# Expert blocks of 128 rows in three float32r passes, with weights split slice by slice into a ring

## The chip, the cores and the metric

The kernel runs on one core of one Trainium2 chip. The metric is device microseconds of one execution. Engines are named as in the profile: PE (TensorE) with its weight loads PEld, DVE (VectorE), ACT (ScalarE), POOL (GpSimd), SP (SyncE, which issues most transfers).

## The reference

One layer of an encoder for 1024 tokens of width 1024, all float32: a mixer sub-layer (neighbourhood attention, bidirectional RWKV-7 and pooling, side by side), then a mixture of experts: 32 experts in 4 groups, two per token.

```
u  = layer_norm(x1) * (1 + scale2) + shift2
# 2048 (token, expert) pairs, sorted by expert, padded per expert to blocks
hb = silu(xb @ w_gate[e]) * (xb @ w_up[e])      # 1024 -> 512, one expert per block
yb = (hb @ w_down[e]) * wt                      # 512 -> 1024, wt = router weight
f  = segment_sum(yb)                            # two rows of y for each token
x  = layer_norm(ALPHA * x1 + gate2 * f) * gain + bias
```

## The kernel before

The program has three parts. The mixer and the router (to about 958 us) are laid out by a scheduler. The expert stage (to about 1540) and the last stage (to the end) are written by hand, each engine with its own program and semaphores, in `experts` and `tail_plan`.

**The expert stage** works through blocks of one expert's tokens. A block holds up to 128, 64 or 32 rows; its size (3, 2 or 1, and 0 behind the last) is read from `m_code` at run time (L1499), and `by_size` (L1513) puts each piece of code in three `If`s, one per size. In this input 37 blocks run: 14 of 128 rows, 5 of 64, 18 of 32. Two blocks of 128 rows follow each other at four places; the others stand between smaller ones. `go_on` (L1523) branches out of the program behind the last block, from the sixteenth on.

The order on every engine is that of `pipeline`: for block g the head of g, the rows of g+1, the down product of g-1, the turn of g.
- *Rows*: POOL gathers a block's rows of u by index into one of NX = 4 buffers `m_xg` (L1612). PE transposes them (L1655); ACT and DVE each move one half into `m_xT` (`evac_T`, L1721).
- *Head*: PE forms gate and up products in `m_pgu`, for 128 rows in two halves of 256 columns (L1672), for smaller blocks several parts of the array at a time (L1680). ACT takes SiLU (L1748, L1751), DVE multiplies (L1772, L1776).
- *Turn*: PE transposes h (L1688), ACT copies it to `m_hT` (L1756).
- *Down*: PE forms `m_py` (L1700, L1711). DVE multiplies by the channel's gate (`out`, L1734, L1739) into one of NY = 3 buffers, and POOL scatters the rows to `ys` (L1620). The router's weight comes in later.

SP loads the three weight matrices of each block (2 MB each) into one of NB = 3 buffers `w`, where the expert changes, gated on the head (semaphore `gu1`) and the down product (`y1`) of the block three before. Behind the last block `finish` loads x1, gain and bias; when POOL has seen its scatters land it signals `done`, and SP then loads `ys`.

**The last stage** has eight tiles of 128 tokens. For each, PE adds two rows of `ys`, weighted by diagonal matrices `dg`, and ALPHA*x1 by a third diagonal, 12 records a tile (L1804). Even tiles get their variance by DVE's `bn_stats` (L1813), odd ones by ACT's copies with sums and squares (L1834, L1841); L1817 is the mean, L1821 and L1826 the small steps to the scale, L1849 and L1852 the normalisation, and DVE applies gain and bias (L1829, L1830). SP writes each tile out.

In the mixer a float32r split already exists: ACT casts a weight tile to `w_h` (L189), DVE subtracts for `w_l` (L190), and three products follow (L196 to L198).

Of the kernel before, what the change touches and what calls it, by code (L numbers as in the profile page):

```python
# [18 lines left out]
D = 1024  # L19
# [8 lines left out]
NB, NPRE, NX, NY, NP = 3, 3, 4, 3, 50  # L28
# [5 lines left out]
def _consts():  # L34
# [18 lines left out]
    add("alpha", np.float32(ALPHA) * np.eye(128))  # L53
# [70 lines left out]
class Builder:  # L124
# [905 lines left out]
    def phase3(self, p3, wo, mk, ps):  # L1030
        nc, tc, I, C = self.nc, self.tc, self.I, self.C
        rows = self.rows
        with ExitStack() as ctx:

            def first(x, **k):
                p = ctx.enter_context(tc.tile_pool(name=f"w{x}", bufs=1, reuse_waits="tile", **k))
                w = p.tile([128, 3 * 4096 + x * D], F32, name=f"w{x}")
                self.placed.append(w.tensor.concrete_tensor().ap())
                return self.expert_views(w[:, 0:12288].rearrange("p (i n) -> p i n", i=3))
# [421 lines left out]
    def experts(self):  # L1461
# [7 lines left out]
        g2 = sb("m_g2", [128, D])  # L1469
        ls = sb("m_ls", [128, 8, 20])  # L1470
# [6 lines left out]
        xT = sb("m_xT", [128, 8, 128])  # L1477
        sil = sb("m_sil", [128, 512])
        junk = wd[2][:, 0]
        h = sb("m_h", [128, 512])  # L1480
        hT = sb("m_hT", [128, 512])
# [5 lines left out]
        names = ["T0", "T1", "xT", "gu0", "gu1", "sil", "h", "ht", "hs", "y0", "y1", "e0", "e1", "late", "g2", "done", "o"]  # L1487
# [57 lines left out]
        def wait(e, name, v):  # L1545
            if v:
                e.wait_ge(sem(name), v)

        tail = self.tail_plan(sem, yall, x1a, of, ls, gain, bias, [(pgu[0], pgu[1]), tuple(pT), tuple(py)], junk)
        with nc.Block() as blk:  # L1550
            @blk.sync
            def _(e):
# [9 lines left out]
                def finish(g):  # L1562
# [6 lines left out]
                    wait(e, "gu1", g - (g - 2) % NB + 1)  # L1569
                    for i, w in enumerate((wg[2], wu[2])):  # L1570
                        e.dma_start(w.rearrange("p (t k) n -> p t (k n)", k=2),
                                    self.x1d[512 * i:512 * i + 512, :].rearrange("(t p) d -> p t d", p=128)
                                    ).then_inc(sem("x1" + "ab"[i]), 16)

                def step(g):
# [5 lines left out]
                    else:  # L1581
# [4 lines left out]
                        wait(e, "gu1", max(g - NB + 1, 0))  # L1586
# [10 lines left out]
                e.wait_ge(sem("done"), 1)  # L1597
                for tt in range(8):
                    e.dma_start(yall[tt], self.ys_d[256 * tt:256 * tt + 256, :].rearrange("(t j) n -> t j n", j=2)
                                ).then_inc(sem(f"l{tt}"), 16)  # L1600
# [6 lines left out]
            def _(e):  # L1607
# [19 lines left out]

                def step(g, c):
                    rows_out(g, c[0])
                    if g + NX < NP:  # L1630
                        c = c + [size(e, g + NX)]

                        def refill():
                            wait(e, "T1", g + 1)
                            gather(g + NX, c[NX])
                        if_any(e, c[NX], g + NX, refill)
# [3 lines left out]
                for g in range(NX):  # L1640
                    c.append(size(e, g))
                    gather(g, c[g])
                step(0, c)
                e.sem_inc(sem("done"), 1)

            @blk.tensor
            def _(e):
# [14 lines left out]

                def head(g, t):
                    b, n = g % NB, g // NB + 1
                    e.wait_ge(sem("xT"), 2 * g + 2)
                    e.wait_ge(sem(f"G{b}"), 16 * n)
                    e.wait_ge(sem(f"U{b}"), 16 * n)
                    if t == 128:
                        for q in range(2):
                            for w, o in ((wg[b], 0), (wu[b], 256)):  # L1670
                                for k in range(8):
                                    i = mm(pgu[q][:, o:o + 256], xT[:, k], w[:, k, 256 * q:256 * q + 256],  # L1672
                                           start=k == 0, stop=k == 7)
                            i.then_inc(sem(f"gu{q}"), 1)
                    else:
                        n = 8 * t
                        e.sem_inc(sem("gu0"), 1)
# [3 lines left out]
                        i.then_inc(sem("gu1"), 1)  # L1681
# [9 lines left out]
                def down(g, t):  # L1691
# [4 lines left out]
                    e.wait_ge(sem(f"D{b}"), 16 * (g // NB + 1))  # L1696
                    if t == 128:
                        for f in range(4):
                            for nh in range(2):
                                i = mm(py[nh], hT[:, 128 * f:128 * f + 128], wd[b][:, f, 512 * nh:512 * nh + 512],  # L1700
                                       start=f == 0, stop=f == 3)
                                if f == 3:
                                    i.then_inc(sem(f"y{nh}"), 1)
                    else:
                        n = 8 * t
                        for a in range(64 // t):
                            for j in range(n // 128):
                                f = a * n // 128 + j
                                for o in range(0, 128, t):
                                    c = o // t * n  # L1710
                                    i = mm(py[0][o:o + t, 0:n], hT[:, 64 * j + t * a:64 * j + t * a + t],  # L1711
                                           wd[b][:, f, c:c + n], start=f == 0, stop=f == 3)
                                    if f == 3 and o in (64 - t, 128 - t):
# [5 lines left out]
            def evac_T(e, g, t, hf):  # L1719
                e.wait_ge(sem(f"T{hf}"), g + 1)  # L1720
                (e.tensor_copy if hf else e.copy)(  # L1721
                    xT[:, 4 * hf:4 * hf + 4, 0:t],
                    pT[hf][:, 0:4 * t].rearrange("p (k t) -> p k t", k=4)).then_inc(sem("xT"), 1)

            def out(e, g, t, q):
# [9 lines left out]
                else:  # L1735
                    n = 8 * t
                    for j in range(64 * q // t, 64 * (q + 1) // t):
                        c = slice(n * j, n * j + n)
                        i = e.tensor_mul(y[0:t, g % NY, c], py[0][t * j:t * j + t, 0:n], g2[0:t, c])  # L1739
                i.then_inc(sem(f"e{q}"), 1)  # L1740

            @blk.scalar
            def _(e):
                def head(g, t):
                    if t == 128:
                        for q in range(2):
                            e.wait_ge(sem(f"gu{q}"), g + 1)
# [214 lines left out]
```

## Time and profile before

| | |
|---|---|
| median of 3 runs | 1604.96 us (1597.93 to 1606.82) |
| the profiled execution | 1608.36 us, its span 1606.5 us |
| granted clock of PE, mean | 0.915 |
| busy share: PE, PEld, DVE, ACT, POOL | 87%, 63%, 48%, 36%, 24% |
| mixer and router | 0 to 958 us |
| expert stage | 958 to 1540 us |
| last stage | 1540 to 1606.5 us |

Times are of the one profiled execution. A record of a matmul is one pass over the array; an f32 product has more records than matmuls in the code (L1672: 32 matmuls, 64 records), a float32r product one each. The clock is given as a share of the upper one of two levels (1.2 and 2.4 GHz).

### The profile page before, as it was taken

How to read it: one execution, taken by the hardware profiler on the slowest of the kernel's cores; microseconds unless marked ns; L12 is line 12 of the kernel's file. 1: busy time of each engine (PE TensorE's matmuls, PEld its weight loads, DVE VectorE, ACT ScalarE, POOL GpSimd, SP SyncE). 2: the span in 40 equal slices, each digit the busy share in tenths (PEclk: the TensorE clock that was granted, in tenths of full speed). 3: DMA queues.
4: the chain of work that ended last, by engine and by line, in shares of the span. 5: the costliest groups of instructions: out<-in, count | busy, mean ns of one | idle time of the engine just before them, and what ended most of it. 6: DMA issues, size and time to landing. Idle time of an engine off the chain costs nothing. (4 is left out here: it accounts for less than half of the span.)

```text
span 1606.5 us, 25830 instructions
## 1 busy us (share of the span) xinstructions
PE 1393.4 (87%) x8662; PEld 1016.2 (63%) x8662; DVE 776.4 (48%) x1999; ACT 571.9 (36%) x1200; POOL 378.6 (24%) x442
## 2 busy tenths in 40 slices
PE   6989999979869899898999738998998798799756
PEld 5778777756556677676788625665764574576322
DVE  6776787845964656665668851111111111111116
ACT  5763342415475667676444320010101000000014
POOL 3331233350446115602223140111111001010000
PEclk8999999987769899989999659999999899999978
DMA  9868899766313217117282659876988866896862
GB/s 254 228 207 299 289 303 350 255 231 179 116 49 105 66 41 203 39 52 229 95 320 106 249 191 351 319 286 249 410 308 331 363 278 255 329 375 265 316 262 107
DMA packets 163400, 371.93 MB, mean 232 GB/s; under 512 B 22881, under 2 KB 99010, under 8 KB 154228
## 3 DMA queue, kind: packets, MB, share of 16 engines
q1 hardware_dynamic: 155555, 350.59, 61.1%
q0 software_dynamic: 7632, 18.51, 3.6%
q8 instruction: 133, 2.18, 0.5%
q14 instruction: 80, 0.65, 0.1%
HBM read 365.47 MB, written 65.44 MB: 268 GB/s over the span
## 5 line engine op out<-in xcount | busy, mean ns | idle before, releaser
L1672 PE MATMUL m_pgu<-w,m_xT 128*128 128x256 f32 x896 | 200.1, 384 | 9.1 <-issue 9.0
L1672 PEld LDWEIGHTS m_pgu<-w,m_xT 128*128 128x128 f32 x896 | 171.2, 192 | 34.2 <-issue 10.7
L1680 PE MATMUL m_pgu<-w,m_xT 128*32 128x256 f32 (+1 forms) x1312 | 118.4, 458 | 39.1 <-issue 38.5
L1620 POOL DMA_INDIRECT ys_s<-m_y,m_idx x37 | 35.0, 947 | 491.7 <-DVE m_y L1739 285.4
L197 PE MATMUL pg<-ul,w_h 128*128 128x512 f32 x320 | 128.2, 401 | 0.2 <-POOL ul L295 0.2
L196 PE MATMUL pg<-uh,w_h 128*128 128x512 f32 x320 | 126.6, 402 | 1.8 <-ACT uh L294 1.1
L198 PE MATMUL pg<-uh,w_l 128*128 128x512 f32 x320 | 126.8, 396 | 0.0
L1680 PEld LDWEIGHTS m_pgu<-w,m_xT 128*32 128x32 f32 (+1 forms) x1312 | 55.5, 126 | 92.3 <-issue 75.3
L1772 DVE TENSOR_TENSOR m_h<-m_sil,m_pgu 128x256 f32<-128x256 f32 x28 | 11.8, 421 | 193.1 <-ACT m_sil L1748 193.1
L1700 PE MATMUL m_py<-w,m_hT 128*128 128x512 f32 x224 | 99.6, 597 | 0.0
L1776 DVE TENSOR_TENSOR m_h<-m_sil,m_pgu 64x256 f32<-64x256 f32 (+1 forms) x23 | 10.8, 470 | 155.9 <-ACT m_sil L1751 155.9
L1748 ACT ACTIVATE m_sil<-m_pgu 128x256 f32<-128x256 f32 x28 | 10.8, 384 | 198.1 <-PE m_pgu L1672 198.1
L210 DVE SCALAR_TENSOR_TENSOR acc<-wm,sc_c,acc 128x256 f32<-128x256 f32 x112 | 62.2, 555 | 30.3 <-DMA wm<-in_w_mod_dram 19.5
L1756 ACT COPY m_hT<-m_ph 128x128 f32<-128x128 f32 (+2 forms) x37 | 14.9, 402 | 168.1 <-PE m_ph L1688 168.1
L1700 PEld LDWEIGHTS m_py<-w,m_hT 128*128 128x128 f32 x224 | 41.4, 190 | 47.3 <-issue 46.9
L196 PEld LDWEIGHTS pg<-uh,w_h 128*128 128x128 f32 x320 | 60.4, 191 | 15.6 <-ACT uh L294 2.0
L197 PEld LDWEIGHTS pg<-ul,w_h 128*128 128x128 f32 x320 | 61.0, 191 | 14.5 <-POOL ul L295 1.0
L198 PEld LDWEIGHTS pg<-uh,w_l 128*128 128x128 f32 x320 | 61.1, 191 | 13.5 <-issue 0.7
L756 PE MATMUL g<-zi,bk 64*128 64x128 f32 x384 | 55.5, 324 | 15.7 <-DMA bk<-bkd 10.0
L945 DVE SCALAR_TENSOR_TENSOR sn<-s,fc,sf 64x64 f32<-64x64 f32 x168 | 47.5, 283 | 43.7 <-PE s L936 40.6
L756 PEld LDWEIGHTS g<-zi,bk 64*128 64x128 f32 x384 | 47.7, 222 | 28.6 <-issue 10.7
L1751 ACT ACTIVATE m_sil<-m_pgu 64x256 f32<-64x256 f32 (+1 forms) x23 | 9.8, 427 | 149.5 <-PE m_pgu L1680 149.5
(534 smaller groups left out, 3101.7 us busy)
## 6 DMA issues: line engine op xcount, KB each, us to landing
w<-in_moe_w_gate_dram SPq DMA_DIRECT2D x37, 2048.0 KB, 8.8
w<-in_moe_w_up_dram SPq DMA_DIRECT2D x37, 2048.0 KB, 13.0
w<-in_moe_w_down_dram SPq DMA_DIRECT2D x37, 2048.0 KB, 15.6
wm<-in_w_mod_dram SPq DMA_DIRECT2D x128, 128.0 KB, 4.5
w<-in_w_in_dram SPq DMA_DIRECT2D x21, 512.0 KB, 6.8
hd<-h SPq DMA_DIRECT2D x18, 512.0 KB, 4.7
wm<-in_w_mod_dram SPq DMA_DIRECT2D x16, 512.0 KB, 6.6
w<-ys_s SPq DMA_DIRECT2D x8, 1024.0 KB, 12.6
```

The source lines that it names most:

```text
L196: mm(out, lh[0], rh[0], start=start, stop=False)
L197: mm(out, lh[0], rh[1], start=False, stop=False)
L198: mm(out, lh[1], rh[0], start=False, stop=stop)
L210: nc.vector.scalar_tensor_tensor(acc, wm, self.sc_c[:, k:k + 1], acc, op0=OP.mult, op1=OP.add)
L756: nc.tensor.matmul(pa[h][:, j], bk[hs, j], zr[hs, j], start=True, stop=True)
L945: nc.vector.scalar_tensor_tensor(sn[H[h], H[h]], p[H[h], 2, H[h]], fc[H[h]], sf[H[h], H[h]], op0=OP.mult, op1=OP.add)
L1620: e.indirect_dma_start(out=self.ys_d, out_offset=off(idx[0:t, NP + g:NP + g + 1]), in_=y[0:t, g % NY], in_offset=None, bounds_check=2 * S ...
L1672: i = mm(pgu[q][:, o:o + 256], xT[:, k], w[:, k, 256 * q:256 * q + 256], start=k == 0, stop=k == 7)
L1680: i = mm(pgu[0][o:o + t, 0:n], xT[:, k, 0:t], w[:, k, c:c + n], start=k == 0, stop=k == 7)
L1700: i = mm(py[nh], hT[:, 128 * f:128 * f + 128], wd[b][:, f, 512 * nh:512 * nh + 512], start=f == 0, stop=f == 3)
L1756: e.copy(hT[:, 0:n], ph[:, 0:n]).then_inc(sem("hs"), 1)
L1772: e.tensor_mul(h[:, c], sil[:, c], pgu[q][:, 256:512]).then_inc(sem("h"), 1)
```

## The change

- **Three passes.** In blocks of 128 rows x, h and the weights are split into a high part (a float32r cast) and the rest. PE multiplies hi by hi, lo by hi and hi by lo (`passes`, L1754 and L1757), 512 columns at a time. Blocks of 64 and 32 rows are computed as before.
- **The ring.** The head's weights are split in eight slices H0 to H7 (one 128-row part of gate and of up, 2 x 512 columns), the down weights in four, D0 to D3. ACT casts a slice to `m_rh`, DVE subtracts for `m_rl` (`slices`); the ring has RING = 3 places, given out in the order of use. `split_pipeline` is the order of ACT and DVE: for step g, H3 to H7 of g, D0 to D2 of g-1, the head's SiLU or product, the rows of g+1, D3 of g-1, H0 and H1 of g+1, the output of g-1, H2 of g+1, the turn. `free` is what a place waits for. PE keeps the order of before.
- **Rows and h.** For 128 rows ACT moves both halves of the rows (high), DVE subtracts for both (low). SiLU waits for the whole head. DVE subtracts for h's low part, `m_hTl`.
- **Buffers and gates.** NX goes from 4 to 2 and NY from 3 to 2; two tiles move into columns of the constants; one tile of the mixer's layout is smaller, so the scheduler lays that part out anew. SP gates weight loads on `fH`, eight counts a block. POOL's refill is issued ahead of the scatter.
- **The last stage.** SP waits for the scatters itself and issues the loads of `ys` in `finish`. In six of the eight tiles PE leaves ALPHA*x1 out, and DVE adds it with the row sums (L1940); tiles 2 and 5 keep PE's third product and ACT's sums. All tiles take the variance from ACT's squares.

```diff
-NB, NPRE, NX, NY, NP = 3, 3, 4, 3, 50
+NB, NPRE, NX, NY, NP = 3, 3, 2, 2, 50
+RING, WX = 3, 192
...
+        def part(g, H, k):
+            b, r = g % NB, (k if H else 8 + k) % RING
...
+        def free(e, g, H, k, end):
+            if H and k >= RING:
+                wait(e, "fH", 8 * g + k - RING + 1)
+            elif H:
+                wait(e, "fH", 8 * g - 1 + min(k, 1))
+                if k < 2:
+                    wait(e, "fD", 3 * (g - 2) + k + 2)
+                else:
+                    wait(e, "y1", g - 1)
+            elif k == 3:
+                wait(e, "fD", 3 * g + 1)
+            else:
+                wait(e, "fH", 8 * g + 8 if end else 8 * g + 14 + k)
+                if end:
+                    wait(e, "y1", g)
...
+                        free(e, g, H, k, end)
+                        e.copy(hi, w).then_inc(sem("h" + x), 1)
+                    else:
+                        e.wait_ge(sem("h" + x), n)
+                        e.tensor_sub(lo, w, hi.bitcast(F32)).then_inc(sem("l" + x), 1)
...
+                slices(e, g, c, H(3, 4, 5, 6, 7))
+                if g:
+                    slices(e, g - 1, old, Dn(0, 1, 2))
+                by_size(e, c, lambda t: head(g, t))
+                if new is not None:
+                    by_size(e, new, lambda t: rows(g + 1, t))
+                if g:
+                    slices(e, g - 1, old, Dn(3))
+                if new is not None:
+                    slices(e, g + 1, new, H(0, 1))
+                if g and out:
+                    by_size(e, old, lambda t: out(g - 1, t))
+                if new is not None:
+                    slices(e, g + 1, new, H(2))
+                turn(g, c)
...
-                    wait(e, "gu1", g - (g - 2) % NB + 1)
+                    wait(e, "fH", 8 * (g - (g - 2) % NB + 1))
...
+                    for k in range(g - NY + 1, g + 1):
+                        wait(e, f"sc{k % NY}", 16 * (k // NY + 1))
+                    for tt in range(8):
+                        e.dma_start(yall[tt], self.ys_d[256 * tt:256 * tt + 256, :].rearrange("(t j) n -> t j n", j=2)
+                                    ).then_inc(sem(f"l{tt}"), 16)
...
-                e.wait_ge(sem("done"), 1)
...
+                def passes(g, H, k, out, hi, lo, first, last, done):
+                    _, wh, wl = part(g, H, k)
+                    n, x = (8 * g + k + 1, "H") if H else (4 * g + k + 1, "D")
+                    e.wait_ge(sem("h" + x), n)
+                    for l in (hi, lo):
+                        for i in range(2):
+                            mm(out[i], l, wh[:, i], start=first and l is hi, stop=False)
+                    e.wait_ge(sem("l" + x), n)
+                    for i in range(2):
+                        done(i, mm(out[i], hi, wl[:, i], start=False, stop=last))
...
+                    e.wait_ge(sem("fH"), 8 * g + 8)
...
+        inside = lambda tt: tt in (2, 5)
...
+                n = 3 if inside(tt) else 2
...
+                    op("dve", f"sum{h}", tt, [("mm", tt), ("x1" + "ab"[tt // 4], 16)], lambda e, h=h: e.scalar_tensor_tensor(
+                        of[tt][:, hs[h]], x1a[tt][:, hs[h]], ALPHA, pf(tt)[h], op0=OP.mult, op1=OP.add,
+                        accum_out=col(tt, h)))
```

How it moves instructions, at two places of the expert stage. PE, at the start of a step, before: the size is loaded, then three branches choose the head (L1672 for 128 rows, L1680 for 64 and 32).

```order
L1513 UNCONDITIONAL_BRANCH
L1499 TENSOR_LOAD m_code
L1499 ISA x2
L1513 COMPARE_AND_BRANCH
L1672 MATMUL m_pgu<-w_8648,m_xT 128x256 x32
L1513 UNCONDITIONAL_BRANCH
L1513 COMPARE_AND_BRANCH
L1680 MATMUL m_pgu<-w_8648,m_xT 64x512 x16
```

The same place of the change (`m_rh`, `m_rl` are the ring; `m_xT_r`, `m_xTl` the rows' high and low part).

```order
L1518 UNCONDITIONAL_BRANCH
L1504 TENSOR_LOAD m_code
L1504 ISA x2
L1518 COMPARE_AND_BRANCH
L1754 MATMUL m_pgu<-m_rh,m_xT_r 128x512 x2
L1754 MATMUL m_pgu<-m_rh,m_xTl 128x512 x2
L1757 MATMUL m_pgu<-m_rl,m_xT_r 128x512 x2
```

The last three rows come eight times, and their operands now come from the ring, no longer from SP's buffer.

DVE from the start of a step, before: only the products with SiLU and the rows' evacuation stand there.

```order
L1499 TENSOR_LOAD m_code
L1499 ISA x2
L1513 COMPARE_AND_BRANCH
L1772 TENSOR_TENSOR m_h<-m_sil,m_pgu 128x256 x2
L1513 UNCONDITIONAL_BRANCH
```

Now, from the same place on (the first row is H3 to H7, the second D0 to D2 of the block before):

```order
L1594 TENSOR_TENSOR m_rl<-w_8648,m_rh 128x1024 x5
L1581 UNCONDITIONAL_BRANCH
L1581 COMPARE_AND_BRANCH
L1594 TENSOR_TENSOR m_rl<-w_7635,m_rh 128x1024 x3
L1581 UNCONDITIONAL_BRANCH
L1518 COMPARE_AND_BRANCH
L1887 TENSOR_TENSOR m_sil<-m_sil,m_pgu 128x256 x2
```

And later in the step, where the next block's first slices stand around the output products:

```order
L1594 TENSOR_TENSOR m_rl<-w,m_rh 128x1024 x2
L1581 UNCONDITIONAL_BRANCH
L1518 COMPARE_AND_BRANCH
L1843 TENSOR_TENSOR m_y<-m_py,cst 128x512 x2
L1518 UNCONDITIONAL_BRANCH
```

Eight subtractions now stand ahead of the product into h, and H2's subtraction comes only behind the output products.

## Rows read from the trace of the kernel before

**Rows 1.** Us; PE, PEld, DVE, ACT, POOL busy; clock, DMA share, GB/s; expert stage.

```profile
958.00:1540.00 582.00, 521.44 (x3496) 338.97 (x3496) 95.97 (x199) 54.05 (x134) 69.03 (x72) 0.95 0.80 311
```

**Rows 2.** Costliest groups: busy us, mean ns | idle before; PE, 128-row blocks.

```profile
L1672 PE MATMUL m_pgu<-w,m_xT 128*128 128x256 f32 x896 | 200.1, 384 | 9.1 <-issue 9.0
...
L1700 PE MATMUL m_py<-w,m_hT 128*128 128x512 f32 x224 | 99.6, 597 | 0.0
```

**Rows 3.** The chain of waits (start us, us, what), three stretches, expert stage.

```profile
992.85 14.01 PE m_pgu L1672 x64
...
1015.62 0.99 PE m_pT L1655 x8
1016.61 7.06 PE m_py L1700 x16
1023.67 0.27 PE m_ph L1688 x2
1023.94 3.59 PE m_pgu L1680 x64
...
1383.11 1.90 PE m_py L1711 x32
1385.01 0.59 PE m_ph L1688 x4
1385.59 6.48 issue
1392.07 5.09 PE m_pgu L1680 x64
```

**Rows 4.** Branches by line: min/median/max ns, first to last start; PE, ACT.

```profile
L1513 PEldq COMPARE_BRANCH  x447: 68/207/5107, 954.3 to 1531.3; - x149
L1513 ACTq COMPARE_BRANCH  x336: 40/45/50, 954.1 to 1530.6; - x168
...
L1513 PEldq COMPARE_BRANCH  x1: 3228/3228/3228, 1018.5 to 1018.5; - x1
...
L1513 PEldq COMPARE_BRANCH  x1: 5107/5107/5107, 1386.3 to 1386.3; - x1
...
L1523 PEldq COMPARE_BRANCH  x1: 4557/4557/4557, 1498.3 to 1498.3; - x1
```

**Rows 5.** Timeline of PE in the mixer (start us, us), float32r passes.

```profile
299.77 0.40 PE L196 MATMUL pg<-uh,w_h 128*128 128x512 f32 x1
...
301.16 0.40 PE L196 MATMUL pg<-uh,w_h 128*128 128x512 f32 x1
```

**Rows 6.** Lines L189 and L190 of the mixer, the split: ns min/median/max.

```profile
L189 ACT CAST w_h<-w x18: 1032/1048/1058, 60.2 to 302.7; 128x1024 fp32r<-128x1024 f32 x18
...
L190 DVE TENSOR_TENSOR w_l<-w,w_h x18: 1209/1220/1559, 61.4 to 305.8; 128x1024 fp32r<-128x1024 f32 x18
```

**Rows 7.** Groups by line and shape, DVE, expert stage.

```profile
L1734 DVE TENSOR_TENSOR m_y<-m_py,m_g 128x512 f32<-128x512 f32 x28 | 19.4, 692 | 80.4 <-PE m_py L1700 80.4
L1772 DVE TENSOR_TENSOR m_h<-m_sil,m_pgu 128x256 f32<-128x256 f32 x28 | 11.8, 421 | 193.1 <-ACT m_sil L1748 193.1
```

**Rows 8.** Sums by stretch (as rows 1), a head after an idle gap.

```profile
1392.10:1397.10 5.00, 5.00 (x64) 2.61 (x64) 0.00 (x0) 0.00 (x0) 0.00 (x0) 0.71 0.99 395
```

**Rows 9.** DMA issues, expert stage: gathers, count, us to landing.

```profile
m_xg<-u_s,m_idx POOLq DMA_INDIRECT x35, 7.9
```

**Rows 10.** The chain of waits, last stage.

```profile
1542.49 2.62 issue
...
1550.18 8.01 PE m_pgu L1804 x12
...
1583.93 5.15 PE m_pgu L1804 x12
```

**Rows 11.** Groups by line and shape, DVE, last stage.

```profile
L1829 DVE TENSOR_TENSOR w<-w,m_xg 128x1024 f32<-128x1024 f32 x8 | 9.7, 1218 | 0.0
...
L1817 DVE TENSOR_SCALAR m_ls<-m_ls 128x1 f32<-128x1 f32 x4 | 0.9, 214 | 10.3 <-ACT w L1834 10.3
```

More of the change, by code (lines that the diff above doesn't have):

```diff
@@ new lines, in slices @@
+        def slices(e, g, c, which, end=False):
+            if which is None:
+                return
+            with e.If(c == 3):
+                for H, k in which:
+                    w, hi, lo = part(g, H, k)
+                    n = 8 * g + k + 1 if H else 4 * g + k + 1
+                    x = "H" if H else "D"
+                    if e is self.act:
+                        if k == 0:
+                            for y in "GU" if H else "D":
+                                e.wait_ge(sem(f"{y}{g % NB}"), 16 * (g // NB + 1))
+                        free(e, g, H, k, end)
[3 more added lines that the diff above has]
+                        e.tensor_sub(lo, w, hi.bitcast(F32)).then_inc(sem("l" + x), 1)
@@ new lines, in split_pipeline, with step, end @@
+        def split_pipeline(e, rows, head, out, turn):
+            H = lambda *ks: [(1, k) for k in ks]
+            Dn = lambda *ks: [(0, k) for k in ks]
+            def step(g, old, c):
+                new = size(e, g + 1) if g + 1 < NP else None
+                slices(e, g, c, H(3, 4, 5, 6, 7))
[13 more added lines that the diff above has]
+                turn(g, c)
+                def end():
+                    slices(e, g, c, Dn(0, 1, 2, 3), True)
+                    if out:
+                        by_size(e, c, lambda t: out(g, t))
+                go_on(e, g, new, end, lambda k: step(k, c, new))
+            c = size(e, 0)
+            by_size(e, c, lambda t: rows(0, t))
+            slices(e, 0, c, H(0, 1, 2))
+            step(0, None, c)
@@ L1695, in down, with done @@
                     wait(e, "e1", g)
-                    e.wait_ge(sem(f"D{b}"), 16 * (g // NB + 1))
                     if t == 128:
-                        for f in range(4):
[L1699 to L1703, printed above, removed]
+                        e.wait_ge(sem("hl"), g + 1)
+                        def done(f, i, m):
+                            if f == 3:
+                                m.then_inc(sem(f"y{i}"), 1)
+                            elif i:
+                                m.then_inc(sem("fD"), 1)
+                        for f in range(4):
+                            c = slice(128 * f, 128 * f + 128)
+                            passes(g, 0, f, py, hTr[:, c], hTl[:, c], f == 0, f == 3, lambda i, m: done(f, i, m))
                     else:
+                        e.wait_ge(sem(f"D{b}"), 16 * (g // NB + 1))
                         n = 8 * t
@@ L1776, in head, with turn @@
                         e.tensor_mul(h[0:64, 0:n], sil[0:64, 0:n], pgu[0][0:64, 0:n]).then_inc(sem("h"), 2)
[L1778 removed]
+                        e.sem_inc(sem("lH"), 8)
+                def turn(g, c):
+                    with e.If(c == 3):
+                        e.wait_ge(sem("hs"), g + 1)
+                        e.tensor_sub(hTl, ph, hTr.bitcast(F32)).then_inc(sem("hl"), 1)
+                split_pipeline(e, lambda g, t: evac_T(e, g, t), head, lambda g, t: [out(e, g, t, q) for q in range(2)], turn)
+                e.sem_inc(sem("fin"), 1)
                 tail(e, "dve")
@@ new lines, in product, with sums @@
+            op("pe", "mm", tt, [("alpha", 0), ("dg0", tt), ("dg1", tt), (f"l{tt}", 16), ("x1" + "ab"[tt // 4], 16)] + free, f)
+        def sums(tt):
+            for h in range(2):
+                if inside(tt):
+                    op("act", f"sum{h}", tt, [("mm", tt)], lambda e, h=h: e.activation(
+                        of[tt][:, hs[h]], pf(tt)[h], AF.Copy, accum_out=col(tt, h)))
+                else:
+                    op("dve", f"sum{h}", tt, [("mm", tt), ("x1" + "ab"[tt // 4], 16)], lambda e, h=h: e.scalar_tensor_tensor(
+                        of[tt][:, hs[h]], x1a[tt][:, hs[h]], ALPHA, pf(tt)[h], op0=OP.mult, op1=OP.add,
+                        accum_out=col(tt, h)))
@@ L1862, in tail_plan @@
         for tt in range(10):
-            if tt < 8 and even(tt):
-                stats(tt)
             if 0 < tt < 9:
                 rstd(tt - 1)
-            if tt < 8 and not even(tt):
-                stats(tt)
+            if tt < 8:
+                if not inside(tt):
+                    sums(tt)
+                mean(tt)
             if tt > 1:
@@ L1871, in tail_plan @@
         for tt in range(9):
-            if tt < 8 and not even(tt):
-                copies(tt)
-            if tt < 8 and even(tt):
-                deviation(tt)
+            if tt < 8 and inside(tt):
+                sums(tt)
             if tt:
                 normal(tt - 1)
-            if tt < 8 and not even(tt):
+            if tt < 8:
                 deviation(tt)
```

210 lines of the change are left out of this document (105 added, 105 removed).

## The prediction, made before the changed kernel was run

> **What bounds the kernel now.** I read the sums by stretch first, for the expert stage between 958 and 1540 us [rows 1]. TensorE (PE) is busy 521.4 of 582 us there at a granted clock of 0.95; VectorE (DVE) 96.0 and ScalarE (ACT) 54.1; the DMA engines 0.80. So the stage is PE's, and DVE and ACT have room. The change trades PE work for DVE and ACT work, so the question is whether that work can be done in time, not whether there is room on average.
>
> The costliest groups [rows 2] give PE's share in blocks of 128 rows: 896 records of L1672 in 200.1 us and 224 of L1700 in 99.6 us, over 14 blocks (64 and 16 records each).
>
> The chain of waits [rows 3] shows how a step goes. A 128-row head is 14.01 us, the down product 7.06. Then a 32-row head follows 0.27 us later and takes 3.59. Elsewhere, after a 32-row down product, PE stands idle for 6.48 us, and the next 32-row head takes 5.09.
>
> The branches on PE's queue [rows 4] explain that gap. Most take 0.207 us, some take 3 to 5 us; on ACT's queue none exceeds 0.05. The 5.107 us one at 1386.3 lies inside the idle 6.48. The 3.228 us one at 1018.5 lies inside the down product 1016.61 to 1023.67, and the next head starts without a gap. Matmuls were already queued there, so PE's sequencer ran ahead and the branch cost nothing. 13 such long branches, 29 us in all (the first and last of these are in the group), are hidden in down products of 128 rows.
>
> **The change part by part.** *PE's work.* 48 records replace the 64 of a head, 24 the 16 of a down product, each one pass of 512 columns. The mixer runs the same float32r passes at (301.16 - 299.77) / 6 = 0.231 us [rows 5]. Head: 48 x 0.231 = 11.1 for 14.0, so -2.9. Down: 24 x 0.231 = 5.5 for 7.06, so -1.5. Over 14 blocks: **-62 us**. (By the busy sums of [rows 2], with their stretches at a lower clock, it would be 299.7 - 14 x 16.6 = 67.)
>
> *The casts and subtractions.* The mixer's own split shows both: 1.048 us on ACT, 1.220 on DVE for 128x1024 [rows 6]. 12 slices: 14.6 us of DVE per 128-row block. With two products into h (0.42), two for the rows' low half (taken as 0.69, as any 128x512 here), two output products (0.69) and one for h's low part, DVE has 14.6 + 0.84 + 1.38 + 1.38 + 0.69 = 18.9 us per block [rows 6, 7]. PE has 11.1 + 5.5 + transposes of 1.0 + 0.3 [rows 3] = 17.9. So in a run of 128-row blocks DVE sets the pace: 18.9 instead of 14.0 + 7.1 + 1.3 = 22.4, less than PE's own saving. Only 4 pairs of such blocks exist (of 37 blocks 14 have 128 rows, 5 have 64, 18 have 32); elsewhere DVE has a small block's time to itself, but may not use it: a ring of three slices lets it run at most three ahead.
>
> *New waits.* (a) At a 128-row head that follows a small block, the short down product and transposes (1.90 + 0.59) don't cover ACT's rows' evacuation (two of about 0.69) and its first cast (1.05): some 1.0 us for 13 heads, **+13**. (b) DVE's order puts the two output products ahead of slice 2's subtraction: about 0.5 us in 14 heads, **+7**. (c) At the end of a block, slices D0 to D2 wait for slots that are free only when the next block's head is done, D3 stands behind SiLU and the evacuation, and the transposed h waits for DVE's subtractions. Behind a small head's end, D0's low part is there after 1.05 + 1.22 = 2.3 us, where PE's transposes and first two passes end at 2.0; D3's after 2.3 + 2 x 1.22 + 0.42 + 0.69 + 1.22 = 7.1, where PE could use it at 6.4. With hand-overs between three engines about 1.5 us in 14 blocks, **+21**. Together **+41**; between 13 (only the first cast shows) and 60 (DVE's 18.9 on the path of each block, less what it overlaps).
>
> *The cover that goes.* PE's sequencer now waits on a slice's semaphores ahead of every four and every two matmuls. It can be ahead by one slice (six records, 1.4 us, at most) where it was ahead by some 20 records. Each step has 12 to 14 branches of 0.207 us and a load of the next size, 3 us in all; that lay beside a 7.06 us product (14.01 for a head). I take half of it as exposed behind 13 down products of 128 rows, 13 x 1.5 = **+20** (0 to 27). The 13 long branches, 29 us, come on top. About 9 us of them still overlap what is queued: **+20** (0 to 29). The rule that speaks of this is in the Trainium skill, "Runtime: NRT & Kernel Launch", section "Instruction fetch mechanics": the sequencer fetches code in 16 KiB blocks ahead of use, "mostly hidden", but a taken branch outside its window of two pages must wait for a fetch. By "mostly hidden" alone this term would be 0; by the sentence on branches it stays as I put it, and the 5.107 us branch agrees with that.
>
> *Clock.* In the head after the idle 6.48 us the granted clock was 0.71 [rows 8], and that head took 5.09 - 3.59 = 1.5 us more. More short gaps: **+5** (0 to 10).
>
> *The stage:* -62 + 41 + 20 + 20 + 5 = **+24**.
>
> *Priced at nothing:* two gather buffers for four, since a gather takes 7.9 us to land [rows 9] and starts two blocks (14 us or more even for small ones, with their gaps) ahead; two output buffers for three, since a scatter has a step's time to land; weight loads, gated on the head's last product as before; the mixer, whose order is laid out anew by the smaller tile but gets no work: 0, within 8 either way.
>
> *The last stage.* Now PE does 12 records in 5.15 us per 128 tokens [rows 10], 8 times, after a slow first one of 8.01. Six tiles lose a third of the matmuls; six get two DVE additions of 128x512. DVE per tile: 2 x 0.69 + 0.21 (mean) + some 0.3 (two small ones, each below the mean's 0.21) + 2 x 1.22 (gain and bias) = 4.3 us [rows 7, 11], six times, and 4.3 - 1.4 = 2.9 for two others: 32 us where PE had 8 x 5.15 = 41. DVE now sets it, for a gain of up to 9. SP waits for the scatters itself, where 2.62 us went between POOL's last branch and its signal [rows 10]: 2.6 more. I take **-11** of the 11.6, bounds 0 (the end behind DVE grows by what the middle gains) and -16 (the slow first tile shortens too).
>
> *Sum:* 1608.4 + 24 - 11 = 1621 against the profiled execution, which stands 3.4 above the median: **1618 us**.
>
> **The rivals.** *The ring keeps up (faster).* If the matmuls queue well enough that branches stay covered, and only the first cast shows: -62 + 13 + 6 (control) + 15 (long branches) + 2 (clock) - 11 = -37, so 1568. For it: DVE and ACT are idle for 83% and 91% of the stage. Against: three slots are 4.2 us of PE work, and D0 to D2 have no slot until the head ahead of them has ended. It decides if the sum of waits and exposure stays under about 60. *Waits and exposure cancel the gain.* With half of (c) and half of the long branches the stage is -62 + 30 + 20 + 10 + 5 = +3, net -8 with the last stage: 1597, and 1608 with nothing from the last stage. *Everything shows (slower still).* Waits at 60, control 27, long branches 29, clock 10: stage +64, net +53, 1658 at the extreme; the middle between that and my sum is 1638. *The change doesn't do what it says:* the passes would not run at 0.231 in this stage. The mixer's three lines L196 to L198 alternate their operands in the same way [rows 5], so I give it no chance of its own.
>
> **How the numbers follow.** Forecast, 1613 to 1632: 0.43. Everything shows, above 1632: 0.12. Cancels, 1597 to 1613: 0.20. Ring keeps up, below 1597 (centre 1568): 0.25. A measurement of this kernel tells 0.5%, 8 us, from no change. So faster 0.25, same 0.20, slower 0.55. The range, 1580 to 1642, leaves out some 0.14 of the faster case and 0.05 at the top; the forecast's own is 1613 to 1632.
>
> **What would show it.** Right: 128-row heads of 12 to 15 us with gaps of 0.5 to 1.5 us whose release is ACT's cast or DVE's subtraction; PE busy down by about 55 us in the stage while its idle time grows by more; DVE near 96 + 14 x (12 x 1.22 + 2 x 0.69) = 320 us there; gaps of 1 to 4 us ahead of small heads after 128-row blocks, where there were none; a last stage ending 9 to 11 us sooner after the last scatter. Wrong: 128-row blocks that take 17 us or less with no gap at slice 2 or at D0, small heads that start as before, or PE busy not down.

## The result, and the profile after

The changed kernel took 1627.88 us in the median of 4 runs (1626.12 to 1635.06), 1.0152 times the kernel before (95% interval 1.0112 to 1.0192). The forecast was 1618 us, slower; the range was 1580 to 1642. The profiled execution of the changed kernel took 1626.12 us, its span is 1624.3.

The three parts of the program moved like this (PE's first transposition of rows, its last down product, the span's end):

| | before | after | difference | forecast |
|---|---|---|---|---|
| mixer and router | 958.0 | 942.4 | -15.6 | 0, within 8 |
| expert stage | 578.6 | 623.3 | +44.7 | +24 |
| last stage | 69.9 | 58.6 | -11.3 | -11 |

So the sum came out near the forecast partly by luck: two errors had opposite signs. The stage lost some 20 us more than forecast, and the mixer gained some 16 us that I had not counted on. First the sums by stretch over the expert stage after (us; PE, PEld, DVE, ACT and POOL busy, PE's clock, DMA share, GB/s):

```profile
942.40:1566.00 623.60, 503.62 (x3384) 335.50 (x3384) 304.43 (x393) 223.92 (x307) 83.20 (x71) 0.89 0.75 290
```

Against [rows 1], DVE has the work that was forecast (304, forecast 320). PE is busy only 18 us less, while its granted clock fell from 0.95 to 0.89, and it is idle for 120 us, where it was 57 (578.6 - 521.4).

The groups of 64 and 32 rows of the stage before (busy us, mean ns of one | idle before, released by):

```profile
L1680 PE MATMUL m_pgu<-w,m_xT 128*32 128x256 f32 (+1 forms) x1312 | 118.4, 458 | 39.1 <-issue 38.5 <-DVE m_xT L1721 0.6
...
L1711 PE MATMUL m_py<-w,m_hT 128*32 128x256 f32 (+1 forms) x656 | 54.8, 414 | 6.6 <-issue 5.8 <-ACT m_hT L1756 0.8
```

The costliest PE groups of the stage after:

```profile
L1773 PE MATMUL m_pgu<-w,m_xT 128*32 128x256 f32 (+1 forms) x1312 | 133.0, 501 | 70.9 <-issue 70.2 <-DVE m_xT L1832 0.7
L1754 PE MATMUL m_pgu<-m_rh,m_xT_r 128*128 128x512 f32 x224 | 76.4, 425 | 10.8 <-issue 6.1 <-ACT m_rh L1591 4.7
...
L1757 PE MATMUL m_pgu<-m_rl,m_xT_r 128*128 128x512 f32 x224 | 73.3, 410 | 2.5 <-DVE m_rl L1594 1.8 <-issue 0.7
L1809 PE MATMUL m_py<-w,m_hT 128*32 128x256 f32 (+1 forms) x656 | 60.6, 445 | 22.7 <-issue 20.6 <-DVE m_y L1848 2.0
...
L1757 PE MATMUL m_py<-m_rl,m_hT_r 128*128 128x512 f32 x112 | 37.5, 417 | 1.4 <-DVE m_rl L1594 1.4
L1754 PE MATMUL m_py<-m_rh,m_hT_r 128*128 128x512 f32 x112 | 37.5, 417 | 7.1 <-issue 4.3 <-ACT m_rh L1591 2.7
```

Read the last column. What waits for ACT's casts and DVE's subtractions is 4.7 + 1.8 + 1.4 + 2.7 = 10.6 us. The idle time ahead of the products of 64 and 32 rows, which the change leaves alone, went from 39.1 and 6.6 us to 70.9 and 22.7, nearly all "issue": PE waits there for nothing that the profile shows. Their records also became longer, 501 and 445 ns in the mean for 458 and 414. The chain of waits after shows such a gap, at the place of the middle of [rows 3], where the 32-row head followed 0.27 us behind the 128-row down product:

```profile
1006.82 0.47 PE m_py L1757 x2
1007.28 0.33 issue
1007.61 0.33 PE m_ph L1781 x2
1007.94 2.25 issue
1010.19 3.66 PE m_pgu L1773 x64
```

and these two branches on PE's queue (min/median/max ns, first to last start) lie in the gap of 2.25 us:

```profile
L1518 PEldq COMPARE_BRANCH  x2: 207/696/1184, 1008.3 to 1008.5; - x2
```

In other places a gap lies inside a small head, with no instruction of PE's queue in it, as the 2.75 us here (chain of waits, a 32-row head):

```profile
1533.79 1.90 issue
1535.68 0.81 PE m_pgu L1773 x9
1536.49 2.75 issue
1539.25 5.78 PE m_pgu L1773 x55
```

What ends such stalls can be read from the trace's DMA packets. In the stage after, 28 branches on PE's queue take over 1 us, 82 us in all, 42 of them in idle gaps (before: 29 branches, 79 us, 26 in gaps). Each of them, before and after, ends 1.3 to 1.7 us behind the end of a 16 KB packet of the instruction queue, and so do 11 of the 12 idle gaps over 1 us that have next to no instruction of PE's queue in them (25 us; before 7 of 7, 12 us). For the 2.75 us above it is the packet from 1536.84 to 1537.78. So these stalls look like waits for code.

Behind gaps the clock can also be lower, and the same 64 records then take longer. Two 32-row heads after (sums by stretch as above), at a granted clock of 1.00, the upper level, and 0.68, a mixture of the two levels; PE had been idle for 1.22 and for 7.46 us ahead of them:

```profile
1172.63:1176.29 3.66, 3.66 (x65) 2.43 (x65) 0.00 (x0) 0.00 (x0) 1.97 (x2) 1.00 0.64 175
...
1520.51:1525.86 5.35, 5.35 (x65) 2.89 (x65) 0.00 (x0) 0.00 (x0) 0.00 (x0) 0.68 1.04 346
```

**A ledger of the stage.** For each kernel I cut PE's timeline into pieces (from a piece's first record to its last, plus the gap ahead of it) and summed them over the 37 blocks, in us. The columns to the right belong to the experiments below.

| piece with the gap ahead | before | after | n1_noring | c1_lead | h1_heads | h2_tail6 | s_before | s_after | s_n1 |
|---|---|---|---|---|---|---|---|---|---|
| 128-row heads | 208.7 | 183.5 | 167.5 | 228.1 | 174.1 | 182.7 | 196.8 | 177.7 | 154.9 |
| 128-row down products | 98.3 | 96.2 | 80.5 | 98.3 | 98.3 | 98.9 | 98.3 | 89.1 | 80.5 |
| heads of 64 and 32 rows | 156.7 | 203.8 | 176.7 | 202.3 | 158.4 | 146.9 | 107.0 | 110.5 | 144.8 |
| down products of 64 and 32 rows | 60.2 | 82.4 | 63.0 | 63.9 | 81.5 | 58.6 | 54.9 | 53.8 | 53.2 |
| transpositions of rows and h | 54.8 | 57.3 | 54.2 | 62.2 | 56.2 | 53.7 | 61.2 | 60.9 | 52.3 |
| stage | 578.6 | 623.3 | 542.0 | 654.8 | 568.5 | 540.8 | 518.1 | 492.1 | 485.5 |

The 128-row pieces gained 27 us, and everything else lost 72: at the pieces of 64 and 32 rows idle time grew by 48 us and the records by 21, and 3 us went at the transpositions. The change leaves these products of PE as they were. What PE did last ahead of a small piece tells where the loss stands (same sums):

| small piece with the gap ahead | count | before | after | c1_lead | h1_heads | h2_tail6 |
|---|---|---|---|---|---|---|
| heads behind a 128-row down product | 11 | 44.7 | 86.1 | 88.3 | 41.0 | 41.5 |
| other heads | 12 | 111.9 | 117.7 | 113.9 | 117.4 | 105.4 |
| down products behind a 128-row head | 10 | 25.7 | 36.3 | 28.8 | 43.5 | 23.5 |
| other down products | 13 | 34.5 | 46.1 | 35.1 | 37.9 | 35.1 |

Of the 47 us that small heads lost, 41 stand behind 128-row down products.

**The last stage.** Its chain of waits after; [rows 10] answer to it.

```profile
1567.96 3.58 DMA ys_s<-m_y,m_idx
1571.54 0.02 issue
1571.56 0.02 SPq L1552
1571.58 0.04 issue
1571.61 5.35 DMA w<-ys_s
1576.96 0.33 issue
1577.29 6.01 PE m_pgu L1928 x8
1583.31 3.43 PE m_pT L1928 x8
1586.74 5.15 PE m_py L1928 x12
```

SP issues the loads 0.07 us after the last scatter has landed, and the 2.62 us are gone. A tile without the third product takes 3.43 us for 5.15. From 1605 on the chain is DVE's sums, gain and bias.

### The profile page after: what moved, and what is told of

It reads as the page before. It is cut to its first block, busy times and chain, and to the rows that moved or that the text cites. A ratio compares the mean times of both kernels' runs of the same rounds, so it can differ in the third digit from the quotient of the medians.

```text
span 1624.3 us, 26572 instructions
## 1 busy us (share of the span) xinstructions
PE 1353.8 (83%) x8526; PEld 999.1 (62%) x8526; DVE 987.9 (61%) x2211; ACT 747.6 (46%) x1379; POOL 390.8 (24%) x442
## 5 line engine op out<-in xcount | busy, mean ns | idle before, releaser
L1594 DVE TENSOR_TENSOR m_rl<-w,m_rh 128x1024 fp32r<-128x1024 f32 x168 | 200.0, 1218 | 137.1 <-ACT m_rh L1591 133.1
L1591 ACT CAST m_rh<-w 128x1024 fp32r<-128x1024 f32 x168 | 172.3, 1050 | 173.9 <-PE m_pgu L1773 90.1
L1773 PE MATMUL m_pgu<-w,m_xT 128*32 128x256 f32 (+1 forms) x1312 | 133.0, 501 | 70.9 <-issue 70.2
L1704 POOL DMA_INDIRECT ys_s<-m_y,m_idx x37 | 48.3, 1305 | 511.7 <-DVE m_y L1848 292.3
L1754 PE MATMUL m_pgu<-m_rh,m_xT_r 128*128 128x512 f32 x224 | 76.4, 425 | 10.8 <-issue 6.1
L1809 PE MATMUL m_py<-w,m_hT 128*32 128x256 f32 (+1 forms) x656 | 60.6, 445 | 22.7 <-issue 20.6
L1891 DVE TENSOR_TENSOR m_sil<-m_sil,m_pgu 64x256 f32<-64x256 f32 (+1 forms) x23 | 10.8, 467 | 107.8 <-ACT m_sil L1865 107.8
L1757 PE MATMUL m_pgu<-m_rl,m_xT_r 128*128 128x512 f32 x224 | 73.3, 410 | 2.5 <-DVE m_rl L1594 1.8
L1754 PE MATMUL m_pgu<-m_rh,m_xTl 128*128 128x512 f32 x224 | 73.4, 410 | 0.4 <-issue 0.4
L756 PEld LDWEIGHTS g<-zi,bk 64*128 64x128 f32 x384 | 44.7, 211 | 26.5 <-ACT am L762 7.6
L1754 PEld LDWEIGHTS m_pgu<-m_rh,m_xT_r 128*128 128x128 f32 x224 | 44.6, 205 | 20.8 <-issue 11.7
```

The costliest lines, as they stand in the source:

```text
L756: nc.tensor.matmul(pa[h][:, j], bk[hs, j], zr[hs, j], start=True, stop=True)
L1591: e.copy(hi, w).then_inc(sem("h" + x), 1)
L1594: e.tensor_sub(lo, w, hi.bitcast(F32)).then_inc(sem("l" + x), 1)
L1704: e.indirect_dma_start(out=self.ys_d, out_offset=off(idx[0:t, NP + g:NP + g + 1]), in_=y[0:t, g % NY], in_offset=None, bounds_check=2 * S ...
L1754: mm(out[i], l, wh[:, i], start=first and l is hi, stop=False)
L1757: done(i, mm(out[i], hi, wl[:, i], start=False, stop=last))
```

## The experiments

Theory A was formed from the result: the passes and the ring do about what was forecast, and the stage lost its time to PE's branches, size loads and code fetches, which the waits on slices uncover, and to the lower clock behind such gaps. Theory B: the casts and subtractions hold PE back.

**e1_rest: the change without the three passes.** The layout, buffers, SP's loads and the last stage of the change, with the products of before:

```diff
-                        for k in range(8):
-                            passes(g, 1, k, pgu, xTr[:, k], xTl[:, k], k == 0, k == 7,
...
+                                    i = mm(pgu[q][:, o:o + 256], xT[:, k], w[:, k, 256 * q:256 * q + 256],
+                                           start=k == 0, stop=k == 7)
```

> The change without the three passes: f32 products, casts and subtractions as before, but the new layout of the mixer, two gather and two output buffers, the loads issued by SP and the new last stage. Both theories expect the expert stage within 8 us of the 578.6 us of before. If the mixer's 15.6 us are due to its new order, it starts the stage near 942 us again, the last stage takes some 58.6 us instead of 69.9, and the time is near 1605 - 15.6 - 11.3 = 1578 us. If the 15.6 us were an accident of one execution: near 1594 us.

Measured: 1586.89 us, 0.9888 of before (0.9835 to 0.994), half-way between the two numbers named. Mixer 945.2, stage 576.1, last stage 58.2 us. So the rest of the change is worth 1.1%, and the three passes alone cost what it gains and more. Over all profiles the mixer ended at 958.0, 961.5 and 964.1 us in the three kernels with the old order, and between 942.4 and 956.1 in the ten with the new one. The gain is real, but the profiled 15.6 us was at its lucky end: the means differ by 11.

**s_after and s_before: the 37 sizes written into the program.** No engine loads a size or branches on one, and the code of the sizes that a block does not have is gone. This works for this input alone and is a measurement, no version to use.

```diff
-            return e.snap(e.value_load(code[0:1, g:g + 1], min_val=0, max_val=3))
+            return KNOWN[g]
...
-                with e.If(c == v):
+                if c == v:
```

> The changed kernel with the 37 block sizes written into the program, so that no engine loads a size or branches on one. Theory A (the stage lost its 45 us to PE's branches, loads and code fetches, which the waits on slices have uncovered, and to the lower clock behind such gaps; the ring itself costs some 12 us): the stage falls from 623 to 550 us or less. Theory B (the casts and subtractions hold PE back): it falls by no more than the kernel before does without branches, to some 580 us.

> The kernel before with the 37 sizes written into the program. Its 64 us of idle gaps in the stage hold 33 us of branches, and more of fetches. Theory A: the stage falls from 578.6 by 35 to 55 us, to some 530, and by less than the changed kernel's, since most branches of before were covered. Theory B: it falls by as much as the changed kernel's.

Measured: 1505.88 us for the changed kernel and 1548.45 for the kernel before, one run each. Sums by stretch over the two stages, the changed kernel first:

```profile
954.00:1446.10 492.10, 457.41 (x3384) 305.89 (x3384) 301.38 (x393) 222.81 (x307) 100.78 (x71) 0.97 0.91 362
```

```profile
961.50:1479.60 518.10, 504.51 (x3496) 330.29 (x3496) 94.18 (x196) 53.84 (x134) 67.68 (x71) 0.98 0.87 343
```

Branches, size loads and the fetches of code that go with them cost the kernel before 60.5 us, a little above theory A's bracket, and the changed one 131. (The 64 us of gaps named for the kernel before take in 7 us ahead of the stage; inside it they are 57.) In the stage 92 and 90 packets of 16 KB on the instruction queue became 28 and 27. Without all this the change is 26 us faster in the stage, with DVE's 301 us still in it. Theory B, which had some 580 for it, cannot give that. The small heads shrink from 157 and 204 us to 107 and 110.

**n1_noring: no ring.** PE makes all passes from one fixed pair of slices, filled with zeros, without waits; ACT and DVE neither cast nor subtract weights.

```diff
-                    _, wh, wl = part(g, H, k)
-                    e.wait_ge(sem("h" + x), n)
+                    wh, wl = fh, fl
...
-                    e.wait_ge(sem("l" + x), n)
```

> The changed kernel with its branches, but without the ring: no casts and subtractions of weights, and PE makes all passes from one fixed pair of slices, without waits on slices (the weights' part of the products is left out). Both theories expect a gain; its size is the price of the ring with all that it uncovers. Theory A: PE's sequencer runs ahead as before, branches are covered again, and the stage is 578.6 - 62 = 517 us, up to 535 with the waits on h's low part; 85 to 105 us are the ring's price. Theory B: the branches stay as uncovered as in the changed kernel, and the stage falls by the waits on slices alone, 30 to 60 us, to 565 or more.

Measured, one run: stage 542.0 us (1547.92 in all). The ring with all that it uncovers costs 81 us, a little below theory A's bracket; the stage itself is above its 535 and below theory B's 565. The ledger divides it. The 128-row pieces gain 59 us against before: that is the passes' own gain, forecast as 62 (if zeros run at the same pace, which was not tested). The ring adds 32 to them (183.5 + 96.2 for 167.5 + 80.5), forecast as 41. Everything else loses 22 us even here, and 50 more with the ring. That the 22 come from shorter 128-row pieces, which cover less, is likely but was not shown.

**s_n1: neither branches nor ring.**

> The changed kernel with the 37 sizes written in and without the ring (PE reads one fixed pair of slices; the weights' part of the products is left out). Set against the changed kernel with the sizes written in (stage 492.1 us) it gives the price of the ring's own waits. Theory A, by the 41 us that the prediction gave to them: stage near 451 us; by the 12 us that the gaps inside the 128-row products show: 480. Theory B: under 430.

Measured, one run: stage 485.5 us, only 6.6 below s_after: close to the second of theory A's numbers, but for another reason. The ledger shows it. The 128-row pieces are 31 us shorter than with the ring, as with branches (32), but now small heads wait for their weights (groups of PE, s_n1):

```profile
L1769 PE MATMUL m_pgu<-w,m_xT 128*32 128x256 f32 (+1 forms) x1312 | 110.5, 436 | 35.1 <-DMA w<-in_moe_w_up_dram 34.5 <-issue 0.5
```

The weights are the next limit: the DMA share of this stage was 0.92.

**c1_lead: the kernel before, with a shorter lead.** All products stay f32, nothing is cast; only PE may no longer queue far ahead at the end of a 128-row piece. (Behind each small piece PE adds one semaphore increment of 0.05 us, to keep the count.)

```diff
+                                    if q and o and k == 7:
+                                        e.wait_ge(sem("oh"), g + 1)
                                     i = mm(pgu[q][:, o:o + 256], xT[:, k], w[:, k, 256 * q:256 * q + 256],
                                            start=k == 0, stop=k == 7)
+                                    if q and o and k == 5:
+                                        i.then_inc(sem("oh"), 1)
...
+                                if f == 3 and nh:
+                                    e.wait_ge(sem("od"), g + 1)
```

> The kernel before, all its f32 work unchanged, with one thing added: ahead of the last matmul of a 128-row head and of a 128-row down product PE waits for its own product two matmuls back, so that its sequencer leaves these pieces with 0.4 to 1.8 us of work queued, as it does behind the last slice of the ring. Nothing else is delayed. Theory A: this alone uncovers branches and fetches; the stage grows from 578.6 by 30 to 71 us (71 is what branches cost the changed kernel beyond what they cost the kernel before: 131 against 60), long branches lie in idle gaps behind 128-row down products, and the clock falls below 0.95. Theory B: under 8 us.

Measured, one run: 1690.97 us, stage 654.8, 76 more (5 above theory A's bracket; theory B had under 8), clock 0.92. The chain of waits of this kernel, at a place like the middle of [rows 3]:

```profile
1024.50 7.06 PE m_py L1707 x16
1031.57 0.27 PE m_ph L1693 x2
1031.83 1.02 issue
1032.86 1.93 PE m_pgu L1684 x31
1034.79 0.46 issue
1035.24 2.13 PE m_pgu L1684 x33
```

The down product is as long as before, 7.06 us, so the wait itself cost nothing there. But the small head behind it no longer starts at once, and it breaks off in the middle. Over the stage the small heads went from 156.7 to 202.3 us; the change made them 203.8. Nearly all of it stands behind 128-row down products, 88.3 us for 44.7 (86.1 in the change). With no work added on ACT or DVE, a lead of a matmul or two reproduces the loss of the small heads. The down products of small blocks hardly moved here (63.9), unlike in the change (82.4); the 128-row heads lost 19 us, half of it idle time and half longer records.

**el_after, el_rest: If and Else in place of three tests.**

```diff
-            for v, t in SIZES:
-                with e.If(c == v):
-                    f(t)
+            with e.If(c == 3):
+                f(128)
+            with e.Else():
+                with e.If(c == 2):
+                    f(64)
+                with e.Else():
...
```

> The changed kernel with the size test as If and Else, nested (128, else 64, else 32), so that PE meets some 8 branches in a step instead of 13; nothing else differs. Theory A: some 1 us of branches a step, of which about half was uncovered: 15 to 40 us less than the changed kernel, near 1600. Theory B: within 8 us of the changed kernel.

> The change without the three passes (1587 us), with the same nested If and Else. Theory A: its branches are covered behind 128-row products and uncovered behind small ones, so it gains less, 5 to 20 us: near 1574. Theory B: within 8 us of 1587.

Measured: el_after 1620.13 us, 1.0071 of before (1.0041 to 1.0102), its stage 607.5 us, 16 less than the change. el_rest 1594.67 us, 0.9918 (0.9884 to 0.9952), where e1_rest had 0.9888: no gain, its stage 7.7 us longer. The first met the low end of theory A's expectation in the stage, but in all it is 7.8 us less than the change, just inside theory B's 8; the second missed it and lies within theory B's 8 us. PE met 371 branches in the stage for 488, 10 a step where I had expected 8, but those over 1 us took 119 us in el_after for the change's 82. Fewer tests alone are no cure.

**h1_heads: three passes in the heads alone.** Down products of 128 rows are f32 again.

```diff
-            Dn = lambda *ks: [(0, k) for k in ks]
+            Dn = lambda *ks: None
...
-                            passes(g, 0, f, py, hTr[:, c], hTl[:, c], f == 0, f == 3, lambda i, m: done(f, i, m))
+                                i = mm(py[nh], hT[:, 128 * f:128 * f + 128], wd[b][:, f, 512 * nh:512 * nh + 512],
+                                       start=f == 0, stop=f == 3)
```

> The changed kernel with the three passes and the ring in the heads of 128 rows alone; down products of 128 rows are f32 again (7.06 us, 16 records, queued without waits on slices), no slices D0 to D3, no low part of h. Theory A: what a small head loses depends on the piece queued ahead of it, so heads of 64 and 32 rows with the gaps ahead of them fall from 204 us back to some 157 to 170 (before: 157), while down products of small blocks, which follow 128-row heads, keep their 82 us (before: 60). Stage: 578.6 - 42 (passes of the heads) + 16 (their ring) + 22 + up to 13 = 575 to 588, 1575 to 1592 us in all. Theory B (the work on ACT and DVE, of which a third goes here, delays the small blocks): small heads stay near 190, the stage near 610.

> The same with the nested If and Else. Theory A: as with the full change, where it gave 16 us in the stage: 5 to 15 us less than with three tests, near 1575. Theory B: no difference beyond 8 us.

Measured: 1580.10 us, 0.9814 of before (0.9756 to 0.9872). Small heads are back at 158.4 us (before 156.7), while small down products stay at 81.5: the ten of the 23 that follow a 128-row head take 43.5 us, for 25.7 before. Both sums were named ahead; the stage, 568.5 us, came out 6.5 below the bracket. The groups of PE in this stage:

```profile
L1769 PE MATMUL m_pgu<-w,m_xT 128*32 128x256 f32 (+1 forms) x1312 | 119.6, 456 | 39.6 <-issue 38.9 <-DVE m_xT L1821 0.7
...
L1800 PE MATMUL m_py<-w,m_hT 128*32 128x256 f32 (+1 forms) x656 | 60.7, 436 | 22.1 <-issue 20.5 <-DVE m_y L1837 1.6
```

With Else (h1_else) it took 1588.11 us, 0.9856 (0.9796 to 0.9916): no gain again, against theory A's expectation.

**h2_tail6: give the lead back.** A head's last two slices are f32 products straight from SP's buffer, so that PE leaves the head with 3.5 us queued.

```diff
-                        for k in range(8):
+                        for k in range(6):
                             passes(g, 1, k, pgu, xTr[:, k], xTl[:, k], k == 0, k == 7,
...
+                        for k in (6, 7):
+                            for i in range(2):
+                                m = mm(pgu[i], xT[:, k], wgu[b][:, i, k], start=False, stop=k == 7)
```

> As the run with three passes in the heads alone, but of a head's eight slices the last two are f32 products from SP's buffer, without casts or waits on slices (8 records of 0.219 us instead of 6 of 0.231 each: 0.37 us more, twice, in 14 heads: 10 us). PE then leaves a 128-row head with 3.5 us queued instead of 0.5. Theory A: down products of small blocks, which follow these heads, fall from 81.5 us (with their gaps) to 60 to 68, and the stage from 568.5 to 555 to 567. Theory B: they stay near 80, and the stage grows to about 575.

Measured: **1550.48 us**, 0.9655 of before (0.9615 to 0.9694), the fastest version here that holds for any input. More PE work made the kernel 30 us faster than h1_heads. The same two groups:

```profile
L1777 PE MATMUL m_pgu<-w,m_xT 128*32 128x256 f32 (+1 forms) x1312 | 114.6, 442 | 33.0 <-issue 32.1 <-DVE m_xT L1834 0.7
...
L1808 PE MATMUL m_py<-w,m_hT 128*32 128x256 f32 (+1 forms) x656 | 54.8, 409 | 5.2 <-issue 3.6 <-DVE m_y L1850 1.6
```

and the stage's sums:

```profile
952.20:1493.00 540.80, 488.84 (x3216) 284.56 (x3216) 195.40 (x294) 139.11 (x237) 94.12 (x71) 0.96 0.85 334
```

Small down products fell from 81.5 to 58.6 us, below theory A's 60 and their 60.2 of before; 128-row heads grew by 8.6 (10 forecast); the clock is at 0.96, for 0.93 in h1_heads. The stage, 540.8, is 14 us below theory A's bracket: small heads gained 11.5 us as well, which I had not expected. The run also takes a quarter of the heads' casts and subtractions away (DVE 195 us for 235), but that is not what the small down products gained by: what they waited for DVE stayed at 1.6 us, and their "issue" went from 20.5 to 3.6.

## Why the prediction was right, and where it was not

*The number* lay in the range partly by luck: the stage was off by 21 us one way, the mixer by 16 the other.

*PE's work, -62*: right. Without the ring the 128-row pieces take 59 us less.

*New waits, +41*: too high for what it names. The ring adds 32 us to the 128-row pieces, with branches (n1_noring) and without (s_n1). With branches 12 of them are idle time, 10.6 released by ACT or DVE, and 20 are longer records, at a clock of 0.92 in the heads for 0.99 without the ring. Without branches 19 are idle time, all released by ACT or DVE, and 12 longer records, at nearly the same clock; why these are longer was not separated further. Of part (c), 21 us, the releasers show only 4.1 ahead of the down product's passes. DVE's place behind the output products and ACT's first cast were seen as named, but smaller: slice 2's subtraction is late in two heads after, by 0.7 and 0.8 us, and by 0.8 to 0.9 in nine of s_after.

*The cover that goes, +20 and +20, and the clock, +5*: the right mechanism, and too small together. All but the 128-row pieces lost 72 us. The two terms for branches were not what was short. Long branches took 26 us of PE's idle time before and 42 after, 17 more for the 20 forecast; all instructions of PE's queue took 38 and 70, so control, with the size loads, added 15 for the 20 forecast. Two things were short. I left out gaps with no instruction of PE's queue in them, in straight code, as at 1536.49: such idle time went from 20 to 50 us, some 11 of it waits for ACT and DVE. And I priced the clock by the few gaps of before: the stage's mean fell from 0.95 to 0.89, and the records of the small pieces alone took 21 us longer.

The Trainium skill ("Runtime: NRT & Kernel Launch", section "Instruction fetch mechanics") calls the cost of crossing from one 16 KiB block of code to the next mostly hidden. The traces agree only as long as matmuls are queued: of 79 us in long branches before, 54 lay beside a busy PE, and the 2.75 us at 1536.49 were not hidden. The same section of the Trainium skill says that a taken branch whose target is outside the current window of two pages forces a fetch. The 28 long branches after, each of which ends behind a 16 KB packet, agree with it, though no run shows where their targets lay.

*The mixer, 0 within 8*: wrong in the profiled execution (-15.6), and on the mean of the profiles (-11) too. A new order from the scheduler can be worth as much as the last stage's edit, and I know of nothing in the trace of before that tells its sign.

*The last stage, -11*: right, by its steps: the 2.62 us went, PE's tiles fell to 3.43, and DVE ends it.

*The rivals.* "The ring keeps up" was nearer to the truth about the ring than the forecast was, and its time was still wrong, because it tied the cover to the ring's waits being short. A wait that costs nothing in itself, as in c1_lead's down product, takes the cover away all the same. Two of the marks that I named failed too: PE's busy time fell by 18 us, not 55 (without the ring, at a clock of 0.94, it fell by 52), and the gaps that ACT or DVE released at 128-row pieces are 10.6 us in all, not 0.5 to 1.5 for each head.

What stays open: what the many branches of 0.2 us cost by themselves, since the runs with the sizes written in took them away together with the fetches. If and Else, with fewer tests, helped in the full change (16 us in the stage) and not in e1_rest and h1_heads. Nor was it told apart why c1_lead spares the small down products, and why the change cost those behind small heads 12 us too (46.1 for 34.5).

## What to carry to other kernels

Matmuls queued ahead of a branch are worth their time: before giving PE faster instructions that wait on semaphores one by one, ask what its sequencer does behind the last of them. Where a fast path needs such waits, end it with a few microseconds of work that waits for nothing; here slower f32 products, 9 us more in the 128-row heads, made the kernel 30 us faster. And take a change apart before judging it: of this one the rest gained 20 us, the heads' passes perhaps 7 more (1580.1 for 1586.9 us, at intervals that overlap), and the down products' passes lost 48.

## What the runs showed of the hardware

One semaphore wait near the end of each 128-row piece of PE, 28 in all, cost a stage of 579 us 76 us (c1_lead, one run). In the down products it was met without delay, and no engine had more to compute. Branches, size loads and fetches cost the kernel before 60 us of its stage, of which the profile's gaps had shown 32 as branches. The 28 and 29 branches of PE's queue over 1 us, after and before, all ended 1.3 to 1.7 us behind a 16 KB packet of the instruction queue; 42 and 26 us of their 82 and 79 lay in idle gaps of PE, the rest beside matmuls that were already queued. A 32-row head of 64 records took 3.66 us at a granted clock of 1.00 and 5.35 at 0.68. With the branches and the ring gone (s_n1), waits for the transfers of weights became the small heads' largest (34.5 us), at a DMA share of 0.92.
